# Gate rows broadcast from one SBUF partition each instead of from DRAM

## The chip, the cores and the metric

The kernel runs on one core of a Trainium2 chip. The metric is device microseconds (us) from launch to end, the median of three runs. A profile is of one further execution, whose own time is given beside its span.

## The reference, cut to what matters

One decoder block on 512 tokens of width 1024, float32, 8 heads of 128 in each of two branches:

```python
u = rmsnorm(x, norm_mix_g)
proj = u @ w_in                       # q,k,v,z,a,b | q,k,v,f | gate_a, gate_b
# branch A: gated delta rule in chunks of 64
beta = sigmoid(gb);  g = -exp(a_log) * softplus(ga + dt_bias);  G = cumsum(g) in a chunk
decay[c, s] = exp(G[c] - G[s])                   (s <= c)
a_mat       = beta[c] * (k k^T) * decay          (s < c), inverted with 1 on the diagonal
attn_intra  = (q k^T) * decay;   q_dec = q * exp(G)
# branch B: softmax attention with a forget bias
cum = cumsum(log_sigmoid(ff + f_bias));  s = q k^T / sqrt(d) + cum[t] - cum[s]
merged = sigmoid(gate_a) * (o_a @ P_A) + sigmoid(gate_b) * (o_b @ P_B)
h = x + merged @ w_out;  out = h + relu(rmsnorm(h) @ w_up)^2 @ w_down
```

Four scalars per head and token come out of the gates: exp(G), beta, G (taken from the middle of a block of 128 tokens), and minus the running sum of the forget logs. Each of them is wanted in two forms: as a column (one value a partition, tokens on partitions), and as a row of 512 tokens that stands the same on all 128 partitions. The rows are what this case is about.

## The kernel before, in words

Every float32 product is made of three fast passes: a matrix is split into a rounded part `hi` (on ScalarE) and a remainder `lo` (on VectorE), and TensorE adds hi*hi, hi*lo and lo*hi. All weights come from DRAM in units of 128x1024 (512 KB), are split on arrival, and are used once. Three buffers hold raw units (`wraw`), four hold the split ones (`whl`); a unit is loaded three ahead of its use, and its load waits until the `lo` of the unit three before it has been computed.

The work before the MLP runs in this order on TensorE: the gate and z projections; for heads 0 to 3 of branch A three projections a head (`project`), with the work of the heads (`head`) between them; projections of branch B (`fox_pair`); heads 4 to 7 of branch A; a stream of the remaining projections. Block inverses, the scan over chunks and the softmax attention (`fox_worker`) are spread between these as coroutines. The order of instructions on each engine is fixed at build time by a scheduler.

The rows. `gates` computes the four scalars as columns in the tile `rows`, [128, 4, 4, 8] (kind, block of 128 tokens, head). One TensorE transpose turns kinds 0 to 2 into [96, 128], one turns kind 3 into [32, 128]; VectorE copies them to SBUF (`rowsT`, `rowsF`), and two DMAs, one on POOL's queue and one on SP's, write them to a DRAM tensor `rowd` [4, 4, 8, 128]. `row_page(kind, h)` then fills a [128, 512] page with one row: a DMA on SP's queue reads the four pieces of 128 values (512 bytes each) from DRAM once for each partition. There are 32 such transfers of 256 KB. Four buffers (`rwp`) hold them.

Who uses a row. In `decays`, rows of kind 2 and 1 of a head are fetched one head ahead: POOL masks kind 2 into `em`, ScalarE takes the exponential of it, POOL multiplies it by kind 1 into `eb`. In `head`, VectorE multiplies k k^T by `eb` (line 642) and k q^T by `em` (line 651), and POOL multiplies q by the row of kind 0 (line 653). `fox_worker` masks the row of kind 3 on POOL.

SP's queue carries, in its fixed order, the weight units, these rows, and the stores of the heads' results to DRAM (`hd`) and their reads back.

Of the kernel before, what the change touches and what calls it, by code (L numbers as in the profile page):

```python
# [7 lines left out]
F32 = mybir.dt.float32  # L8
F32R = mybir.dt.float32r
AF = mybir.ActivationFunctionType  # L10
ALU = mybir.AluOpType
# [4 lines left out]
P = 128  # L16
T = 512
D = 1024
KT = D // P
H = 8  # L20
NCH = T // P
# [22 lines left out]
def hybrid_block(tc, a, out):  # L44
    nc = tc.nc
# [6 lines left out]
    drp = ctx.enter_context(tc.tile_pool(name="drp", bufs=1, space=DRAM))  # L52
    mix = ExitStack()
    cm = mix.enter_context(tc.tile_pool(name="cm", bufs=1))
    rwp = mix.enter_context(tc.tile_pool(name="rwp", bufs=4))
# [10 lines left out]
    def nm(s):  # L66
        n_names[0] += 1
        return f"{s}_{n_names[0]}"
# [5 lines left out]
    def page(dt=F32, s="pg"):  # L74
        if s in FOX_TAGS:
            return fxp.tile([P, T], dt, tag=s, name=nm(s))
        tag = TAGS_OF.get(s, s)
        if tag in TAGS:
            return pgp.tile([P, T], dt, tag=tag, name=nm(s), bufs=TAGS[tag])
        return pgp.tile([P, T], dt, tag="pg", name=nm(s))  # L80
# [3 lines left out]
    def const(shape, s, dt=F32):  # L84
        return (cp if s in KEEP else cm).tile(shape, dt, tag=s, name=s)
# [15 lines left out]
    def atps(s="at"):  # L101
        return pat.tile([P, T], F32, tag="at", name=nm(s))

    def v3(ap, n):
        return ap.rearrange("p (a b) -> p a b", a=n)

    def bc(ap, n):
        return ap.unsqueeze(2).to_broadcast(list(ap.shape) + [n])

    def cs(c):  # L110
        return slice(c * P, (c + 1) * P)

    mm = nc.tensor.matmul
    vec, act, pool = nc.vector, nc.scalar, nc.gpsimd
# [23 lines left out]
    def start(gen):  # L138
        tasks.append(gen)
        return gen  # L140
# [160 lines left out]
    ident = const([P, P], "ident")  # L301
# [52 lines left out]
    def inv_rms(pss, rs, rb):  # L354


        for c in range(NCH):
            vec.tensor_scalar(rs[:, c:c + 1], pss[:, c * 64:c * 64 + 1], 1.0 / D, EPS, op0=ALU.mult, op1=ALU.add)
        rsq(rs, rs)
        yield  # L360
        prb = atps("rb")
        for c in range(NCH):
            mm(prb[:, cs(c)], rs[:, c:c + 1].to_broadcast([P, P]), ident, start=True, stop=True)
        act.copy(rb, prb)
# [21 lines left out]
    for pool_, tag, n in early:  # L386
        t = pool_.tile([P, n * T], F32R, tag=tag, name=nm("xs"))
# [22 lines left out]
    def normalise():  # L410
        for k in range(KT):
            pool.tensor_tensor(xt[k], xt[k], rb, op=ALU.mult)
            split(xt[k], mix_g[:, k:k + 1], dst=(uh(k), ul(k)))
            nc.sync.dma_start(ud[k], xt[k])
            if k % 2:
                yield
# [38 lines left out]
    beta = const([P, NCH, H], "beta")  # L455
    gf = const([P, NCH, 16], "gf")
    ngc = const([P, NCH, H], "ngc")
    kds = const([P, NCH, H], "kds")
    dec = const([P, NCH, H], "dec")
    nbe = const([P, NCH, H], "nbe")  # L460
    cc = const([P, NCH, H], "cc")
    rowd = drp.tile([4, NCH, H, P], F32, tag="rowd", name="rowd")

    def rowc(t):
        return t[:, :].unsqueeze(1).to_broadcast([P, NCH, H])

    def gates(ps):
        abT = page(s="abT")
        act.copy(abT[:64, :], ps[:64, :])
        yield from inv_rms(pss, rs, rb)  # L470
        start(normalise())
        yield
        pt = atps("abt")
        for c in range(NCH):
            mm(pt[:, c * 32:(c + 1) * 32], abT[:64, cs(c)], blk_id[0:64, :], start=True, stop=True)
        ab = const([P, NCH, 32], "ab")
        vec.tensor_tensor(ab, v3(pt[:, 0:NCH * 32], NCH), bc(rs[:, :], 32), op=ALU.mult)
        act.activation(beta, ab[:, :, 8:16], AF.Exp, scale=-1.0)
        aexp = const([P, H], "aexp")
        act.activation(aexp, alog, AF.Exp)  # L480
        yy = const([P, NCH, 16], "yy")
        vec.tensor_tensor(yy[:, :, 0:8], ab[:, :, 0:8], rowc(dtb), op=ALU.add)
        vec.tensor_tensor(yy[:, :, 8:16], ab[:, :, 16:24], rowc(fbias), op=ALU.add)
        vec.tensor_scalar(yy[:, :, 8:16], yy[:, :, 8:16], -1.0, None, op0=ALU.mult)

        ee = const([P, NCH, 16], "ee")
        vec.scalar_tensor_tensor(ee, yy, -1.0, yy, op0=ALU.mult, op1=ALU.min)
        act.activation(ee, ee, AF.Exp)
        yield
        vec.tensor_scalar(beta, beta, 1.0, None, op0=ALU.add)  # L490
        vec.reciprocal(beta, beta)
        zz = const([P, NCH, 16], "zz")
        vec.tensor_scalar(zz, ee, 2.0, None, op0=ALU.add)
        vec.reciprocal(zz, zz)
        vec.tensor_tensor(zz, zz, ee, op=ALU.mult)
        vec.tensor_tensor(ee, zz, zz, op=ALU.mult)
        pp = const([P, NCH, 16], "pp")
        vec.tensor_scalar(pp, ee, 1.0 / 19, None, op0=ALU.mult)
        for k in (17, 15, 13, 11, 9, 7, 5, 3):
            vec.scalar_tensor_tensor(pp, pp, 1.0 / k, ee, op0=ALU.add, op1=ALU.mult)  # L500
        vec.scalar_tensor_tensor(pp, pp, 1.0, zz, op0=ALU.add, op1=ALU.mult)
        vec.tensor_scalar(yy, yy, 0.0, None, op0=ALU.max)
        vec.scalar_tensor_tensor(gf, pp, 2.0, yy, op0=ALU.mult, op1=ALU.add)
        vec.scalar_tensor_tensor(gf[:, :, 0:8], gf[:, :, 0:8], -1.0, rowc(aexp), op0=ALU.mult, op1=ALU.mult)
        vec.tensor_scalar(gf[:, :, 8:16], gf[:, :, 8:16], -1.0, None, op0=ALU.mult)
        yield
        pc = atps("cum")
        mm(pc[:, 0:64], upper, gf[:, :, :].rearrange("p a b -> p (a b)"), start=True, stop=True)
        mm(pc[:, 64:128], ones, gf[:, :, :].rearrange("p a b -> p (a b)"), start=True, stop=True)
        cum = const([P, NCH, 16], "cum")  # L510
        vec.tensor_copy(cum, v3(pc[:, 0:64], NCH))
        mm(pc[:, 128:160], mid, gf[:, :, 0:8], start=True, stop=True)
        tot = const([P, NCH, 16], "tot")
        vec.tensor_copy(tot, v3(pc[:, 64:128], NCH))

        rows = const([P, 4, NCH, H], "rows")
        vec.tensor_copy(rows[:, 2], v3(pc[:, 128:160], NCH))
        act.activation(rows[:, 0], cum[:, :, 0:8], AF.Exp)
        vec.tensor_copy(rows[:, 1], beta)
        pt = atps("rowsT")  # L520
        nc.tensor.transpose(pt[:96, 0:P], rows[:, 0:3, :, :].rearrange("p k c h -> p (k c h)"), ident)
        rowsT = const([96, P], "rowsT")
        vec.tensor_copy(rowsT, pt[:96, 0:P])
        nc.gpsimd.dma_start(rowd[0:3, :, :, :].rearrange("k c h t -> (k c h) t"), rowsT)
        vec.tensor_scalar(ngc, rows[:, 2], -1.0, None, op0=ALU.mult)
        yield
        early_rows[0] = True
        vec.tensor_copy(cc[:, 0], cum[:, 0, 8:16])
        pre = const([P, NCH, H], "pre")
        vec.tensor_copy(pre[:, 1], tot[:, 0, 8:16])  # L530
        for c in range(2, NCH):
            vec.tensor_tensor(pre[:, c], pre[:, c - 1], tot[:, c - 1, 8:16], op=ALU.add)
        vec.tensor_tensor(cc[:, 1:], cum[:, 1:, 8:16], pre[:, 1:], op=ALU.add)
        vec.tensor_scalar(rows[:, 3], cc, -1.0, None, op0=ALU.mult)
        vec.tensor_tensor(kds, tot[:, :, 0:8], cum[:, :, 0:8], op=ALU.subtract)
        act.activation(kds, kds, AF.Exp)
        act.activation(dec, tot[:, :, 0:8], AF.Exp)
        vec.scalar_tensor_tensor(nbe, beta, -1.0, rows[:, 0], op0=ALU.mult, op1=ALU.mult)
        yield
        pt = atps("rowsT")  # L540
        nc.tensor.transpose(pt[:32, 0:P], rows[:, 3, :, :].rearrange("p c h -> p (c h)"), ident)
        rowsF = const([32, P], "rowsF")
        vec.tensor_copy(rowsF, pt[:32, 0:P])
        nc.sync.dma_start(rowd[3, :, :, :].rearrange("c h t -> (c h) t"), rowsF)

    def row_tile(src, v=None):
        t = rwp.tile([P, T], F32, tag="row", name=nm("row"))
        nc.sync.dma_start(v3(t[:, :], NCH) if v else t, src)
        return t

    def row_page(kind, h):
        return row_tile(rowd[kind, :, h, :].partition_broadcast(P), True)


    G = 4
# [57 lines left out]
    def head(h, AT, q, k, v, box, res):  # L613
# [27 lines left out]
        for c in range(NCH):  # L641
            vec.scalar_tensor_tensor(AT[:, hi_ * NCH + c, :], pkk[:, cs(c)], r2[:, c:c + 1], eb[:, cs(c)],
                                     op0=ALU.mult, op1=ALU.mult)
        er = row_page(0, h)
        yield
        pkq = atps("kq")
# [214 lines left out]
    def bias_rows(n):  # L861

        if n < len(fq) and n not in rows_of:
            rows_of[n] = row_page(3, fq[n][0])
        return rows_of.get(n)
# [525 lines left out]
    for k, (w, c, p, s_) in enumerate(MLP):  # L1391
# [6 lines left out]
        n = pos[0]  # L1398
# [122 lines left out]
```

## Time and profile before

| | |
|---|---|
| three runs | 977.39, 977.97, 980.99 us; median 977.97 |
| profiled execution | 979.09 us, span 977.3 us, TensorE clock 1.00 |
| TensorE matmuls | 968.0 us busy, 99% of the span |
| VectorE, ScalarE, GpSimd (POOL) | 73%, 63%, 22% |
| DMA | 176.50 MB, mean 181 GB/s |
| row transfers from DRAM | 32, issued from 69.7 to 358.5 us |

A share is over the whole span, so what counts for the rows is the stretch in which they are fetched: 14 of the 32 are issued between 69 and 121 us, while the first four heads are worked on, and eight between 245 and 272 us, when the second four begin. TensorE's busy time includes the pipelining of matmuls and says whether it had something under way, not how far it is from its peak.

### The profile page before, as it was taken

What the parts mean: (1) busy time and instruction counts of PE and PEld (TensorE: products, weight loads), DVE (VectorE), ACT (ScalarE), POOL (GpSimd) and SP (SyncE); (2) the same over time, 40 slices, a digit from 0 to 9 for tenths busy, and PEclk for the clock granted to TensorE, in tenths of its full rate; (3) what the DMA queues carried; (4) which work ended last, traced back from release to release, by engine and by line L of the source; (5) the groups of instructions that cost most, each with busy time, mean ns of one, the idle gap of its engine ahead of it and who ended that gap; (6) DMA issues with size and microseconds to landing.
All of it is one profiled execution on the core that took longest, in us unless ns stands there. A gap on an engine that the chain in (4) does not pass through costs nothing.

```text
span 977.3 us, 17204 instructions
## 1 busy us (share of the span) xinstructions
PE 968.0 (99%) x6532; PEld 871.9 (89%) x6532; DVE 709.4 (73%) x1206; ACT 617.8 (63%) x1079; POOL 219.5 (22%) x220
## 2 busy tenths in 40 slices
PE   8999999999999999999999999999999999999998
PEld 6788899998888999999998888889989989988986
DVE  6877777656577799855656534889896697698596
ACT  7778654766764787868567412668755765666761
POOL 1503220202313423521320014412121121121110
PEclk9999999999999999999999999999999999999999
DMA  7646872475675987757888726678698888889883
GB/s 267 210 146 191 236 179 88 130 256 175 156 210 163 194 155 169 174 120 175 252 172 234 258 88 191 113 180 173 184 197 192 194 168 203 184 170 205 187 175 110
DMA packets 97634, 176.50 MB, mean 181 GB/s; under 512 B 8160, under 2 KB 53376, under 8 KB 97552
## 3 DMA queue, kind: packets, MB, share of 16 engines
q1 hardware_dynamic: 83088, 122.92, 40.6%
q0 software_dynamic: 14464, 52.49, 30.8%
q8 instruction: 51, 0.84, 0.4%
q14 instruction: 31, 0.25, 0.1%
HBM read 154.34 MB, written 21.04 MB: 179 GB/s over the span
## 4 chain that ended last, share of the span: by engine, by line
PE 91%; ACT 3%; DVE 2%; issue 2%; DMA 1%; POOL 0%; SPq 0%; ACTq 0%; POOLq 0%; DVEq 0%
PE mlp L1172 36%; PE st L1012 13%; PE mm L279 7%; PE mm L276 7%; PE mm L275 7%; PE fx L965 2%; PE fx L962 2%; PE fx L963 2%; PE fo L945 2%; PE sc L920 2%; PE pT L936 1%; ACT hi L256 1%; PE kq L648 1%; PE kk L640 1%; DMA row<-oad 1%
## 5 line engine op out<-in xcount | busy, mean ns | idle before, releaser
L1403 ACT CAST hi<-draw 128x1024 fp32r<-128x1024 f32 x124 | 130.1, 1050 | 118.4 <-PE mlp L1172 101.5
L1410 DVE TENSOR_TENSOR lo<-draw,hi 128x1024 fp32r<-128x1024 f32 x124 | 151.2, 1221 | 44.9 <-ACT hi L1403 42.1
L256 ACT CAST hi<-raw 128x1024 fp32r<-128x1024 f32 (+1 forms) x62 | 62.7, 1020 | 77.6 <-PE mm L276 48.6
L1172 PE MATMUL mlp<-hi,shi 128*128 128x512 f32 x280 | 109.5, 391 | 0.1
L1172 PE MATMUL mlp<-hi,slo 128*128 128x512 f32 x280 | 109.1, 390 | 0.0
L1172 PE MATMUL mlp<-lo,shi 128*128 128x512 f32 x280 | 109.0, 389 | 0.0
L257 DVE TENSOR_TENSOR lo<-raw,hi 128x1024 fp32r<-128x1024 f32 (+1 forms) x62 | 75.4, 1222 | 28.3 <-ACT hi L256 13.6
L1172 PE MATMUL mlp<-slo,hi 128*128 128x256 f32 x448 | 90.3, 283 | 0.0
L1172 PE MATMUL mlp<-shi,lo 128*128 128x256 f32 x448 | 90.3, 283 | 0.0
L1172 PE MATMUL mlp<-shi,hi 128*128 128x256 f32 x448 | 90.3, 283 | 0.0
L276 PE MATMUL mm<-ulo,hi 128*128 128x512 f32 x216 | 84.9, 394 | 1.2 <-DVE ulo L290 1.2
L275 PE MATMUL mm<-uhi,hi 128*128 128x512 f32 x216 | 85.2, 396 | 0.0
L257 DVE TENSOR_TENSOR lo<-sraw,hi 128x1024 fp32r<-128x1024 f32 x49 | 61.6, 1257 | 23.5 <-ACT hi L256 20.1
L1172 PEld LDWEIGHTS mlp<-shi,hi 128*128 128x128 f32 x448 | 70.6, 192 | 0.9
L256 ACT CAST hi<-sraw 128x1024 fp32r<-128x1024 f32 x49 | 51.3, 1047 | 30.7 <-PE st L1012 14.8
L1172 PEld LDWEIGHTS mlp<-shi,lo 128*128 128x128 f32 x448 | 69.9, 192 | 0.0
L1172 PEld LDWEIGHTS mlp<-slo,hi 128*128 128x128 f32 x448 | 69.8, 192 | 0.0
L1172 PEld LDWEIGHTS mlp<-hi,shi 128*128 128x128 f32 x280 | 52.6, 188 | 11.1 <-issue 0.7
L1172 PEld LDWEIGHTS mlp<-lo,shi 128*128 128x128 f32 x280 | 52.6, 188 | 11.1
L1172 PEld LDWEIGHTS mlp<-hi,slo 128*128 128x128 f32 x280 | 52.6, 188 | 10.3
L600 DVE SCALAR_TENSOR_TENSOR conv<-mm,c_conv,conv 128x511 f32<-128x511 f32 (+2 forms) x72 | 53.5, 744 | 5.6 <-ACT conv L597 4.4
L279 PE MATMUL mm<-uhi,lo 128*128 128x512 f32 x216 | 57.1, 402 | 0.0
(337 smaller groups left out, 2389.7 us busy)
## 6 DMA issues: line engine op xcount, KB each, us to landing
draw<-w_u POOLq DMA_DIRECT2D x32, 512.0 KB, 6.0
draw<-w_d POOLq DMA_DIRECT2D x32, 512.0 KB, 6.0
sraw<-w_st POOLq DMA_DIRECT2D x28, 512.0 KB, 6.0
draw<-w_d SPq DMA_DIRECT2D x26, 512.0 KB, 4.3
raw<-w_gdn SPq DMA_DIRECT2D x24, 512.0 KB, 4.3
draw<-w_u SPq DMA_DIRECT2D x24, 512.0 KB, 4.5
sraw<-w_st SPq DMA_DIRECT2D x21, 512.0 KB, 5.2
hd<-hd SPq DMA_DIRECT2D x34, 256.0 KB, 5.5
```

What stands on the lines that cost most here:

```text
L256: act.copy(hi[:, c], raw[:, c])
L257: vec.tensor_tensor(lo[:, c], raw[:, c], hi[:, c].bitcast(F32), op=ALU.subtract)
L275: mm(o, w, rhi(k), start=(k == 0), stop=False)
L276: mm(o, w, rlo(k), start=False, stop=False)
L279: mm(o, lo[:, k * cols:(k + 1) * cols], rhi(k), start=False, stop=(k == KT - 1))
L600: vec.scalar_tensor_tensor(y[:, s:], ps[:, :T - s], cw[:, i:i + 1], y[:, s:], op0=ALU.mult, op1=ALU.add)
L920: mm(psc[:, :n], qT[:, s], kT[:, :n], start=True, stop=True)
L945: mm(po[:, cs(i)], vt[c], st[i][:, cs(c)], start=(c == 0), stop=(c == i))
L1012: mm(o, u, w, start=first and t == 0 and k == 0 and j == 0 and x is hi, stop=x is lo and k == 3, skip_group_check=True)
L1172: return (lambda *args, **kw: tc.keep_in_program_order(f(*args, **kw))) if self.pinned[0] else f
L1403: pact.copy(hi, raws[m][0])
L1410: pvec.tensor_tensor(lo, raws[m][0], hi[:, :].bitcast(F32), op=ALU.subtract)
```

## The change

Each row becomes one partition of one SBUF tile. `rows` is laid out [128, 4, 32] (block, kind and head); `rows_out` makes four transposes for a set of kinds, one a block, into the four column blocks of one PSUM page, and one VectorE copy brings them to the tile `rowf` [40, 512]: partitions 0 to 23 hold kinds 0 to 2, partitions 32 to 39 kind 3. `row_page` reads a row from its partition of `rowf` with a step of 0 over 128 copies. The DRAM tensor and its two writing DMAs go. The small tiles of `gates` move into one page of the shared page pool, which makes room for `rowf`.

```diff
-    rowd = drp.tile([4, NCH, H, P], F32, tag="rowd", name="rowd")
+    rows = const([P, NCH, 4 * H], "rows")
+    rowf = const([40, T], "rowf")
+
+    def rows_out(kinds, p0):
+        n, k0 = len(kinds) * H, kinds[0] * H
+        pt = atps("rowsT")
+        for c in range(NCH):
+            nc.tensor.transpose(pt[:n, cs(c)], rows[:, c, k0:k0 + n], ident)
+        vec.tensor_copy(rowf[p0:p0 + n, :], pt[:n, :])
...
-        ab = const([P, NCH, 32], "ab")
+        tmp = page(s="gates")
+        ab = v3(tmp[:, 0:P], NCH)
+        yy, ee, zz, pp, cum, tot = [v3(tmp[:, P + 64 * i:P + 64 * i + 64], NCH) for i in range(6)]
...
-        pt = atps("rowsT")
-        nc.tensor.transpose(pt[:96, 0:P], rows[:, 0:3, :, :].rearrange("p k c h -> p (k c h)"), ident)
-        rowsT = const([96, P], "rowsT")
-        vec.tensor_copy(rowsT, pt[:96, 0:P])
-        nc.gpsimd.dma_start(rowd[0:3, :, :, :].rearrange("k c h t -> (k c h) t"), rowsT)
+        rows_out((0, 1, 2), 0)
...
-        pt = atps("rowsT")
-        nc.tensor.transpose(pt[:32, 0:P], rows[:, 3, :, :].rearrange("p c h -> p (c h)"), ident)
-        rowsF = const([32, P], "rowsF")
-        vec.tensor_copy(rowsF, pt[:32, 0:P])
-        nc.sync.dma_start(rowd[3, :, :, :].rearrange("c h t -> (c h) t"), rowsF)
+        rows_out((3,), 32)
...
     def row_page(kind, h):
-        return row_tile(rowd[kind, :, h, :].partition_broadcast(P), True)
+        n = (kind if kind < 3 else 4) * H + h
+        t = rwp.tile([P, T], F32, tag="row", name=nm("row"))
+        nc.sync.dma_start(t, rowf[n:n + 1, :].unsqueeze(1).to_broadcast([1, P, T]))
+        return t
```

On SP's queue, where the first rows are fetched, there stood before (`rowd` is the DRAM tensor, `raw` a weight unit, `hd` a store of a head's results):

```order
L227 DMA raw_903<-w_gdn 128x1024
L544 DMA rowd<-rowsF 32x128
L548 DMA row_616<-rowd 128x4x128
L548 DMA row_618<-rowd 128x4x128
L548 DMA row_818<-rowd 128x4x128
L548 DMA row_820<-rowd 128x4x128
L227 DMA raw_983<-w_gdn 128x1024
L148 DMA hd_592<-kn_748 128x4x128
```

and stands now (`rowf` is the SBUF tile):

```order
L227 DMA raw_899<-w_gdn 128x1024
L549 DMA row_612<-rowf 128x1x512
L549 DMA row_614<-rowf 128x1x512
L549 DMA row_814<-rowf 128x1x512
L549 DMA row_816<-rowf 128x1x512
L227 DMA raw_979<-w_gdn 128x1024
L148 DMA hd_588<-kn_744 128x4x128
L148 DMA hd_588<-vb_798 128x4x128
```

The write to DRAM is gone from the queue; the rows keep their places between the weights and the stores, here and in the rest of the queue. On POOL's queue the other write (`rowd<-rowsT`) is gone and nothing else has moved.

On TensorE, in the projection before the first rows (`mm` is that product, `ktm` the first head's transposes), there stood before:

```order
L276 MATMUL mm_714<-ulo_190,hi_634 128x512
L521 MATMUL rowsT_471<-ident,rows 96x128
L275 MATMUL mm_714<-uhi_183,hi_634 128x512
L276 MATMUL mm_714<-ulo_191,hi_634 128x512
L275 MATMUL mm_714<-uhi_184,hi_634 128x512
L276 MATMUL mm_714<-ulo_192,hi_634 128x512
L541 MATMUL rowsT_539<-ident,rows 32x128
L119 MATMUL ktm_731<-ident,conv_665 128x128 x4
```

and stands now:

```order
L276 MATMUL mm_710<-ulo_190,hi_630 128x512
L469 MATMUL rowsT_465<-ident,rows 24x128 x4
L275 MATMUL mm_710<-uhi_183,hi_630 128x512
L469 MATMUL rowsT_534<-ident,rows 8x128 x4
L276 MATMUL mm_710<-ulo_191,hi_630 128x512
L275 MATMUL mm_710<-uhi_184,hi_630 128x512
L276 MATMUL mm_710<-ulo_192,hi_630 128x512
L119 MATMUL ktm_727<-ident,conv_661 128x128 x4
```

Eight transposes stand where two stood, all before the same head's transposes.

More of the change, by code (lines that the diff above doesn't have):

```diff
@@ L480, in gates @@
         act.activation(aexp, alog, AF.Exp)
-        yy = const([P, NCH, 16], "yy")
         vec.tensor_tensor(yy[:, :, 0:8], ab[:, :, 0:8], rowc(dtb), op=ALU.add)
@@ L484, in gates @@
         vec.tensor_scalar(yy[:, :, 8:16], yy[:, :, 8:16], -1.0, None, op0=ALU.mult)
-        ee = const([P, NCH, 16], "ee")
         vec.scalar_tensor_tensor(ee, yy, -1.0, yy, op0=ALU.mult, op1=ALU.min)
@@ L491, in gates @@
         vec.reciprocal(beta, beta)
-        zz = const([P, NCH, 16], "zz")
         vec.tensor_scalar(zz, ee, 2.0, None, op0=ALU.add)
@@ L496, in gates @@
         vec.tensor_tensor(ee, zz, zz, op=ALU.mult)
-        pp = const([P, NCH, 16], "pp")
         vec.tensor_scalar(pp, ee, 1.0 / 19, None, op0=ALU.mult)
@@ L509, in gates @@
         mm(pc[:, 64:128], ones, gf[:, :, :].rearrange("p a b -> p (a b)"), start=True, stop=True)
-        cum = const([P, NCH, 16], "cum")
         vec.tensor_copy(cum, v3(pc[:, 0:64], NCH))
         mm(pc[:, 128:160], mid, gf[:, :, 0:8], start=True, stop=True)
-        tot = const([P, NCH, 16], "tot")
         vec.tensor_copy(tot, v3(pc[:, 64:128], NCH))
[L516 to L519, printed above, removed]
-        pt = atps("rowsT")
-        nc.tensor.transpose(pt[:96, 0:P], rows[:, 0:3, :, :].rearrange("p k c h -> p (k c h)"), ident)
-        rowsT = const([96, P], "rowsT")
-        vec.tensor_copy(rowsT, pt[:96, 0:P])
-        nc.gpsimd.dma_start(rowd[0:3, :, :, :].rearrange("k c h t -> (k c h) t"), rowsT)
-        vec.tensor_scalar(ngc, rows[:, 2], -1.0, None, op0=ALU.mult)
+        vec.tensor_copy(rows[:, :, 2 * H:3 * H], v3(pc[:, 128:160], NCH))
+        act.activation(rows[:, :, 0:H], cum[:, :, 0:8], AF.Exp)
+        vec.tensor_copy(rows[:, :, H:2 * H], beta)
+        rows_out((0, 1, 2), 0)
+        vec.tensor_scalar(ngc, rows[:, :, 2 * H:3 * H], -1.0, None, op0=ALU.mult)
         yield
@@ L533, in gates @@
         vec.tensor_tensor(cc[:, 1:], cum[:, 1:, 8:16], pre[:, 1:], op=ALU.add)
-        vec.tensor_scalar(rows[:, 3], cc, -1.0, None, op0=ALU.mult)
+        vec.tensor_scalar(rows[:, :, 3 * H:], cc, -1.0, None, op0=ALU.mult)
         vec.tensor_tensor(kds, tot[:, :, 0:8], cum[:, :, 0:8], op=ALU.subtract)
@@ L537, in gates @@
         act.activation(dec, tot[:, :, 0:8], AF.Exp)
-        vec.scalar_tensor_tensor(nbe, beta, -1.0, rows[:, 0], op0=ALU.mult, op1=ALU.mult)
+        vec.scalar_tensor_tensor(nbe, beta, -1.0, rows[:, :, 0:H], op0=ALU.mult, op1=ALU.mult)
         yield
-        pt = atps("rowsT")
-        nc.tensor.transpose(pt[:32, 0:P], rows[:, 3, :, :].rearrange("p c h -> p (c h)"), ident)
-        rowsF = const([32, P], "rowsF")
-        vec.tensor_copy(rowsF, pt[:32, 0:P])
-        nc.sync.dma_start(rowd[3, :, :, :].rearrange("c h t -> (c h) t"), rowsF)
+        rows_out((3,), 32)
     def row_tile(src, v=None):
```

## The prediction

> **What bounds the kernel now.** I read the page's list of busy times first, then the waits, then the stretches in which rows are fetched.
>
> ```profile
> PE 968.0 (99%) x6532; PEld 871.9 (89%) x6532; DVE 709.4 (73%) x1206; ACT 617.8 (63%) x1079; POOL 219.5 (22%) x220
> PE 91%; ACT 3%; DVE 2%; issue 2%; DMA 1%; POOL 0%; SPq 0%; ACTq 0%; POOLq 0%; DVEq 0%
> ```
>
> TensorE has something under way for 968.0 of 977.3 us, and the chain of waits stands on it for 91%. A cheaper row can shorten the kernel only where TensorE waits for a row, or for something behind one. TensorE's list of waits, longest first, begins so:
>
> ```profile
> PE mm L276 <- DVE ulo L290: 1.2, 2, 0.7
> PE mm L402 <- ACT xs L289: 1.1, 2, 0.6
> PE warm L305 <- DVE expo L300: 1.1, 1, 1.1
> ```
>
> Nothing in it is longer, and nothing of it hangs on a row. So there is next to nothing to win, and the question is what cover the row transfers have. The stretches of 10 us in which the first heads are worked on (engine columns, then the clock, the share of the DMA engines' time, GB/s):
>
> ```profile
> core 0: us, PE busy (x) PEld busy (x) DVE busy (x) ACT busy (x) POOL busy (x), PEclk, DMA share, GB/s
> 70.00:80.00 10.00, 10.00 (x51) 8.39 (x51) 7.20 (x14) 7.98 (x27) 1.91 (x3) 1.00 0.33 99
> 90.00:100.00 10.00, 10.00 (x56) 8.55 (x55) 7.73 (x15) 8.54 (x19) 5.70 (x6) 1.00 0.91 202
> 110.00:120.00 10.00, 10.00 (x56) 8.53 (x55) 8.52 (x20) 3.04 (x6) 0.97 (x2) 1.00 0.89 238
> ```
>
> TensorE is full throughout, but the DMA engines reach 0.9. What stands on SP's queue there, from the DMA issues of 69 to 121 us (count, size, median us to landing), with the rates in 40 slices of that stretch:
>
> ```profile
> GB/s 57 58 87 65 71 86 158 149 130 143 161 295 310 347 183 238 93 138 231 207 348 225 201 138 182 330 313 243 118 147 215 334 344 308 147 63 113 220 374 393
> row<-rowd SPq DMA_DIRECT2D x14, 256.0 KB, 8.8
> raw<-w_fox SPq DMA_DIRECT2D x6, 512.0 KB, 8.5
> ```
>
> The weights that TensorE needs stand in one queue with 14 rows. How near they already are to being late, ScalarE's waits from 60 to 130 us say, and then the wait in its timeline; behind it VectorE's remainder of that unit and TensorE's first use of the pair of units that it belongs to:
>
> ```profile
> ACT hi L256 <- DMA raw<-w_fox: 6.9, 2, 5.5
> 120.67 1.05 ACT L256 CAST hi<-raw 128x1024 fp32r<-128x1024 f32 x1 [5.46 <-DMA raw<-w_fox]
> 121.75 1.23 DVE L257 TENSOR_TENSOR lo<-raw,hi 128x1024 fp32r<-128x1024 f32 x1 [1.16 <-ACT hi L256]
> 134.70 0.36 PE L962 MATMUL fx<-hi,uhi 128*128 128x256 f32 x1
> ```
>
> ScalarE stood 5.46 us for that weight. Its split ended at 121.75 + 1.23 = 122.98, TensorE takes it up at 134.70: 11.7 us of cover are left, and no more. That figure is the hinge of the whole case.
>
> **The change part by part.** *The row transfer* is the part that counts, 32 times. What it takes now: in 70:80 the four first rows are all but alone on the queue, 99 GB/s x 10 us = 0.99 MB, 3.8 rows of 0.262 MB, or 2.6 us a row, with the engines only a third busy. The changed one moves the same 256 KB to the same 128 partitions in 128 pieces of 2 KB instead of 512 of 512 bytes, which by itself could only be quicker. But all 128 pieces are read from one partition, and no row of this trace reads so. Bounds, from the nearest rows:
>
> ```profile
> out<-acc SPq DMA_DIRECT2D x8, 256.0 KB, 2.0
> rowd<-rowsF SPq DMA_DIRECT2D x1, 16.0 KB, 1.5
> ```
>
> Below: `out<-acc` reads 256 KB of SBUF out of all 128 partitions, and takes 2.0 us where 16 KB take 1.5, so 0.5 us for the bytes. That is the price if a partition can be read as fast as all of them together. Above: the best rate of the slices, 393 GB/s, is what 16 engines get together; if one partition gives no more than one engine's share, 393 / 16 = 24.6 GB/s, a row takes 262 KB / 24.6 = 10.7 us.
>
> [...]
>
> Between 0.5 and 10.7 I take the upper mechanism, since 128 reads of the same bytes differ from `out<-acc` in just that, but with two rows under way at a time: rows next to each other on the queue come from different partitions (kind 2 of head 0 from 16, kind 1 from 8, then 17 and 9), and the queue has several transfers in flight, as 8.8 us to landing at 2.6 us a row shows. That is 10.7 / 2 = 5.3 us a row, 2.7 more than now.
>
> *First heads.* The late weight above was issued at 112.36; these are the first and the last rows issued ahead of it, 14 in all:
>
> ```profile
> 69.71 2.04 SPq L548 DMA_DIRECT2D row<-rowd  x4
> 110.26 2.01 SPq L548 DMA_DIRECT2D row<-rowd  x1
> 112.36 0.64 SPq L227 DMA_DIRECT2D raw<-w_fox  x1
> ```
>
> 14 x 2.7 = 37.8 us later, less 11.7 of cover: TensorE stands 26.1 us. The rows themselves are as late, and POOL already waits for them (its waits on rows, all the run: 7.7 for `conv`, 6.4 for `em`, 3.7 for `eb`):
>
> ```profile
> POOL conv L653: 7.7, 2
> POOL em L583: 6.4, 4
> POOL eb L589: 3.7, 1
> ```
>
> Behind a late `eb` VectorE stands at line 642, with the next `lo` and the convolutions queued behind it. This runs beside the late weights, in the same queue and by the same amount, so I count the larger alone.
>
> *Second heads.* From 245.8 to 271 us eight rows are issued. The first and the last of them, and the stretches:
>
> ```profile
> 245.84 0.46 SPq L548 DMA_DIRECT2D row<-rowd  x1
> 271.06 0.36 SPq L548 DMA_DIRECT2D row<-rowd  x1
> ...
> 240.00:260.00 20.00, 20.00 (x106) 17.08 (x105) 8.22 (x10) 11.81 (x20) 8.56 (x8) 1.00 0.55 159
> 260.00:280.00 20.00, 19.87 (x101) 16.35 (x100) 13.57 (x21) 17.53 (x40) 4.88 (x5) 1.00 0.84 208
> ```
>
> 8 x 2.7 = 21.6 us more, against 20 x (0.45 + 0.16) = 12.2 us in which the DMA engines have nothing to do, and the same 11.7 of cover, since the weights run equally far ahead: 0. The other 10 rows stand about 18 us apart or more, but for a last pair: 0.
>
> *The detour through DRAM* goes. Its two writes took 1.9 us (`rowsT`) and 1.5 us (`rowsF`, above) to land, and the first row was issued 1.3 us after the second:
>
> ```profile
> rowd<-rowsT POOLq DMA_DIRECT2D x1, 48.0 KB, 1.9
> L524 POOL DMA_DIRECT2D rowd<-rowsT x1: 629/629/629, 67.8 to 67.8; - x1
> L544 SPq DMA_DIRECT2D rowd<-rowsF x1: 339/339/339, 68.4 to 68.4; - x1
> L521 PE MATMUL rowsT<-ident,rows x1: 272/272/272, 64.8 to 64.8; 128*96 128x128 f32 x1
> L523 DVE COPY rowsT<-rowsT x1: 277/277/277, 67.2 to 67.2; 96x128 f32<-96x128 f32 x1
> ```
>
> About 1 us earlier for the first row, which the longer copies take back: 512 columns instead of 128 at 277 ns, at most 4 x 0.28 = 1.1 us for each of two, on VectorE, which is 72% busy there. Were that cover gone, it would be 1.7 us. *Transposes:* six more on TensorE, in a stretch where it is full. One is 0.27 us alone; in a row of its kind it takes less, as eight matmuls of 128x128 on the chain show:
>
> ```profile
> 78.43 0.89 PE kk L640 x8
> ```
>
> 0.89 / 8 = 0.11, so 6 x 0.11 = 0.7 us on the path. *The gates' small tiles in one page:* the same instructions on other addresses, 0; one page of 53 is held until the gates are done, and the order on the engines shows nothing that moved for it.
>
> The sum, on the profiled execution's 979.09 us: 979.1 + 26.1 + 0.7 = 1005.9. That execution lies 1.1 us above the median of the runs, so 1005 us.
>
> **The rivals.** *One row after the other.* If the engines take a queue's pieces strictly in order, the second partition is not read before the first is done, and a row costs 10.7 us, 8.1 more. First heads 14 x 8.1 - 11.7 = 101.7; second 8 x 8.1 - 12.2 - 11.7 = 40.9; in all 979.1 + 101.7 + 40.9 + 0.7 - 1.1 = 1121 us. For it: 16 engines with eight pieces each, all at one door. Against it: a queue that already has three or four transfers in flight. [...]
>
> *No limit at one partition.* If 2.6 us come from the number of pieces (the engines are a third busy at 512 pieces a row), and a partition is read as fast as needed, 128 pieces take a quarter, about 0.7 us, and the queue empties. TensorE was not waiting, so nothing is won by it: 979.1 + 0.7 - 1.1 = 979 us. This side decides up to a price of 2.6 + 11.7 / 14 = 3.4 us a row, the point at which the cover is used up. For it: the low share in 70:80. Against it: the reads all go to one place.
>
> *Faster* than that would need time that TensorE now loses where the rows are fetched:
>
> ```profile
> 60.00:380.00 320.00, 319.87 (x2306) 289.90 (x2306) 233.14 (x516) 211.09 (x453) 80.06 (x73) 1.00 0.66 175
> ```
>
> It is idle for 320.00 - 319.87 = 0.13 us there; 5 us would have to come from elsewhere, and I see no place.
>
> **How the numbers follow.** Half a per cent, 5 us, is about what a measurement of this kernel tells from no change. The bounded price with rows overlapping, 1005, anywhere from 988 to 1040: 0.42. One after the other, 1040 to 1121: 0.30. No limit, 973 to 983: 0.24, of which 0.20 within half a per cent and 0.04 faster. The last 0.04 is for a small loss between 983 and 988. So faster 0.04, same 0.20, slower 0.42 + 0.30 + 0.04 = 0.76. The range runs from 976, the no-limit case, to 1090, most of the serial one, and leaves out less than 2 in 10. The forecast's own range is 988 to 1040.
>
> **What would show it.** Right: rows that land over 15 us after issue in the first heads, with the engines' share near 1 at a rate of under 100 GB/s; ScalarE's casts (line 256) waiting for `raw` for tens of us; TensorE waiting between 80 and 140 us and hardly from 240 to 280; the rest of the span as long as before. Rival one: DMA-bound in both stretches, some 40 us lost in the second. Wrong altogether: landings under 5 us, and TensorE full from 70 to 130 us.

## The result, and the profile after

The changed kernel takes 1118.49 us (median of 4 runs, 1112.95 to 1119.34), the kernel before 978.17 us beside it: a ratio of 1.1417, 95% interval 1.1373 to 1.1461. The prediction had the direction, but 140 us are lost where it had 27, and the time lies outside its range. The profiled execution took 1117.67 us, with a span of 1115.9.

Busy times, the granted clock in 40 slices, and the chain of waits by engine and by line, of the changed kernel:

```profile
PE 995.6 (89%) x6538; PEld 892.1 (80%) x6538; DVE 705.9 (63%) x1206; ACT 616.3 (55%) x1079; POOL 218.3 (20%) x219
PEclk9998685899998789898999999999999999999999
PE 67%; DMA 19%; DVE 6%; ACT 4%; SPq 2%; issue 1%; POOL 0%; ACTq 0%; POOLq 0%; DVEq 0%
PE mlp L1170 31%; PE st L1010 9%; DMA row<-rowf 9%; DMA sraw<-w_st 4%; PE mm L279 4%; PE mm L276 4%; PE mm L275 4%; DMA raw<-w_fox 3%; PE fx L960 2%; PE fx L961 2%; PE fx L963 2%; DVE conv L598 1%; DMA hd<-kn 1%; DVE lo L257 1%; PE fo L943 1%
```

TensorE was 99% busy and is 89% busy. Transfers were 1% of the chain and are 19%, first among them the rows, then two kinds of weights. Two things happened to TensorE: it stands idle 1115.9 - 995.6 = 120.3 us where it stood 9.3, and the same work keeps it busy 27.6 us longer (968.0 to 995.6), at a granted clock that falls below full speed from 84 to 223 us and again from 335 to 530.

Where in the program it is lost shows in the last start of three groups of TensorE's matmuls (the two times are the first and the last start): `fx` ends the stretch of the first heads, `kk` that of the second heads, `mlp` is the last stage. Before:

```profile
L962 PE MATMUL fx<-hi,uhi x192: 277/283/368, 121.1 to 210.3; 128*128 128x256 f32 x192
L640 PE MATMUL kk<-conv x64: 270/275/275, 78.3 to 338.6; 128*128 128x128 f32 x64
L1172 PE MATMUL mlp<-hi,shi x280: 387/389/487, 616.9 to 972.7; 128*128 128x512 f32 x140
```

After:

```profile
L960 PE MATMUL fx<-hi,uhi x192: 278/283/562, 159.6 to 288.2; 128*128 128x256 f32 x192
L638 PE MATMUL kk<-conv x64: 270/275/421, 78.1 to 452.4; 128*128 128x128 f32 x64
L1170 PE MATMUL mlp<-hi,shi x280: 387/389/487, 755.4 to 1111.2; 128*128 128x512 f32 x140
```

At the end of the first heads the kernel is 288.2 - 210.3 = 77.9 us late, at the end of the second 113.8 (35.9 more), when the last stage begins 138.5 (24.7 more), and at its end still 138.5. The same three stretches by engine, before and then after (TensorE's busy time is the first number behind the length; the clock and the DMA engines' share stand last but two and last but one):

```profile
60.00:210.30 150.30, 150.30 (x1226) 138.55 (x1226) 106.30 (x241) 96.73 (x207) 31.13 (x28) 1.00 0.61 174
210.30:338.60 128.30, 128.17 (x752) 111.64 (x751) 89.60 (x178) 81.87 (x182) 37.88 (x34) 1.00 0.68 179
338.60:616.90 278.30, 277.83 (x2096) 255.93 (x2095) 178.52 (x358) 167.80 (x308) 71.92 (x65) 1.00 0.69 178
```

```profile
60.00:288.20 228.20, 159.04 (x1229) 144.53 (x1229) 104.78 (x240) 96.23 (x207) 30.91 (x27) 0.84 0.80 113
288.20:452.40 164.20, 138.07 (x753) 118.19 (x751) 85.81 (x175) 78.43 (x177) 37.01 (x34) 0.91 0.86 128
452.40:755.40 303.00, 285.43 (x2095) 262.66 (x2094) 179.66 (x361) 170.18 (x311) 71.93 (x65) 0.97 0.70 169
```

In the first stretch TensorE is idle for 228.20 - 159.04 = 69.2 us, and its own work is 159.04 - 150.30 = 8.7 us longer; in the second 26.1 and 9.9, in the third 17.6 and 7.6. The DMA engines are busier while they move less: 0.80 at 113 GB/s where it was 0.61 at 174.

Two of the stretches of 10 us that the prediction showed of before, now:

```profile
70.00:80.00 10.00, 10.00 (x52) 8.40 (x51) 7.69 (x14) 6.28 (x22) 2.33 (x2) 1.00 0.91 37
90.00:100.00 10.00, 1.91 (x9) 1.25 (x7) 5.15 (x10) 3.26 (x6) 1.63 (x1) 0.73 0.88 127
```

In the first, the four first rows are fetched: 99 GB/s at a share of 0.33 has become 37 GB/s at 0.91. TensorE still has work then; from 90 to 100 us it has 1.91 us of it.

The transfers of 69 to 210 us (share of the 16 engines in tenths, GB/s in 40 slices of 3.5 us, then the rows and one kind of weights with the median us to landing):

```profile
DMA  9897797899898987998989879899999889889999
GB/s 31 26 55 35 73 50 72 209 86 27 184 30 82 51 25 170 34 37 158 31 26 192 31 137 52 25 28 27 27 150 53 25 217 43 27 136 241 366 120 28
row<-rowf SPq DMA_DIRECT2D x14, 256.0 KB, 18.1
raw<-w_fox SPq DMA_DIRECT2D x7, 512.0 KB, 13.0
```

Eighteen of the 40 slices lie under 40 GB/s (25 to 37, mean 28.9) with the engines' share at 0.7 to 0.9: that is the rate of a row by itself (26 to 28 in runs below). In the slices of 150 and more between them weights and stores move. At 27 GB/s a row of 262 KB takes 9.7 us.

How a late row reaches TensorE, by the waits behind which most is lost. ScalarE's waits for two weights, one after the other, and behind the second TensorE's for ScalarE:

```profile
177.15 1.04 ACT L256 CAST hi<-raw 128x1024 fp32r<-128x1024 f32 x1 [26.43 <-DMA raw<-w_fox]
198.44 1.04 ACT L256 CAST hi<-raw 128x1024 fp32r<-128x1024 f32 x1 [19.13 <-DMA raw<-w_fox]
199.39 0.63 ACT L600 ACTIVATE conv<-conv 128x512 f32<-128x512 f32 x1
200.07 1.12 PE L119 MATMUL ktm<-ident,conv 128*128 128x128 f32 x4 [37.34 <-ACT conv L600]
```

and the chain of waits between 60 and 240 us, three of its longest pieces (start, us, what):

```profile
68.47 18.93 DMA row<-rowf
...
153.75 23.33 DMA raw<-w_fox
...
184.61 13.75 DMA raw<-w_fox
```

The rows hold POOL, which masks them (`em`, `eb`, with waits of up to 9.10 and 9.81 us for a row in the first heads); ScalarE's exponentials follow POOL; the weights stand on SP's queue among the rows, and ScalarE, whose order is fixed, stands at a cast (line 256) with the activation of the next head's `conv` (line 600) behind it: VectorE's part of that `conv` (line 598) had ended at 181.06 + 1.52 = 182.58 us, and the activation began at 199.39. TensorE stops at that head's transposes (`ktm`), not at the projection that the weight is for. In the third stretch the chain runs through the weights `w_st`. Late rows are on their way at the same time on SP's queue, but only the second of these three weights was issued there; the first and the third were issued on POOL's queue, which carries no rows:

```profile
442.63 16.23 DMA sraw<-w_st
...
472.47 12.47 DMA sraw<-w_st
...
488.95 21.14 DMA sraw<-w_st
```

### The profile page after: what moved, and what is told of

Its sections match the earlier page's. It is cut to its first block, busy times and chain, and to the rows that moved or that the text cites. A ratio compares the mean times of both kernels' runs of the same rounds, so it can differ in the third digit from the quotient of the medians.

```text
span 1115.9 us, 17208 instructions
## 1 busy us (share of the span) xinstructions
PE 995.6 (89%) x6538; PEld 892.1 (80%) x6538; DVE 705.9 (63%) x1206; ACT 616.3 (55%) x1079; POOL 218.3 (20%) x219
## 4 chain that ended last, share of the span: by engine, by line
PE 67%; DMA 19%; DVE 6%; ACT 4%; SPq 2%; issue 1%; POOL 0%; ACTq 0%; POOLq 0%; DVEq 0%
PE mlp L1170 31%; PE st L1010 9%; DMA row<-rowf 9%; DMA sraw<-w_st 4%; PE mm L279 4%; PE mm L276 4%; PE mm L275 4%; DMA raw<-w_fox 3%; PE fx L960 2%; PE fx L961 2%; PE fx L963 2%; DVE conv L598 1%; DMA hd<-kn 1%; DVE lo L257 1%; PE fo L943 1%
## 5 line engine op out<-in xcount | busy, mean ns | idle before, releaser
L256 ACT CAST hi<-raw 128x1024 fp32r<-128x1024 f32 (+1 forms) x62 | 62.7, 1020 | 135.1 <-DMA raw<-w_fox 51.8
L119 PE MATMUL ktm<-ident,conv 128*128 128x128 f32 x32 | 6.9, 355 | 69.9 <-ACT conv L600 69.9
L279 PE MATMUL mm<-uhi,lo 128*128 128x512 f32 x216 | 66.1, 451 | 0.0
L119 PEld LDWEIGHTS ktm<-ident,conv 128*128 128x128 f32 x32 | 4.8, 179 | 72.0 <-ACT conv L600 71.6
```

The source lines that it names most:

```text
L256: act.copy(hi[:, c], raw[:, c])
L279: mm(o, lo[:, k * cols:(k + 1) * cols], rhi(k), start=False, stop=(k == KT - 1))
```

## The experiments

Each kernel is the changed one with the edit shown; lines that only declare tiles or lay out the transposes are left out. Ratios are to the kernel before on the same chip.

**Is it the source partition?** Everything of the change stays, the piece size of 2 KB too, but the tile is written to DRAM and the rows are read from there.

```diff
-        vec.tensor_copy(rowf[p0:p0 + n, :], pt[:n, :])
+        vec.tensor_copy(rowf[p0:p0 + n, :], pt[:n, :])
+        (nc.sync if p0 else nc.gpsimd).dma_start(rowd[p0:p0 + n, :], rowf[p0:p0 + n, :])
...
-        nc.sync.dma_start(t, rowf[n:n + 1, :].unsqueeze(1).to_broadcast([1, P, T]))
+        nc.sync.dma_start(t, rowd[n, :].partition_broadcast(P))
```

> The change with one thing undone: rowf (40 rows of 2 KB) is written to DRAM, and each row is read from there, in 128 pieces of 2 KB. Transposes, the page of the gates and the size of the pieces stay as in the change; only the source is DRAM again. If the one source partition is the cause: within 5 us of the kernel before (978), the first four rows at 2.6 us each or less. If the size or number of the pieces, or one of the other edits, costs the time: 1100 us or more.

Measured: 978.99 us, ratio 1.0006 (0.9997 to 1.0016). The first rows while nothing else moves, in the kernel before and then in this one:

```profile
71.00:77.00 6.00, 6.00 (x30) 4.97 (x29) 4.58 (x11) 4.00 (x14) 1.69 (x2) 1.00 0.29 79
```

```profile
72.00:76.00 4.00, 4.00 (x21) 3.30 (x20) 2.84 (x8) 2.75 (x12) 2.59 (x2) 1.00 0.58 137
```

So the six transposes, the layout of the gates and the new page cost nothing that can be measured, and the whole loss is in reading one partition. The run says a second thing: at 137 GB/s a row takes 262 KB / 137 = 1.9 us where the kernel before, with 512-byte pieces at 79 GB/s, pays 3.3, and nothing is won by it, as TensorE was not waiting. (The prediction's 2.6 us come from 70 to 80 us, in which the first pieces of a weight move too. The 0.8 us that two expectations below give a row of this kernel is the rate of 76 to 78 us, 325 GB/s, of which a part is a weight as well.)

**Has each partition a limit of its own?** Each row is laid on 16 partitions, and its 128 reads are spread over them: on neighbours (16 h to 16 h + 15), or 8 apart (h, h + 8, ...). POOL makes the copies ahead of the transposes; three pages fewer make room.

```diff
+            x = page(s="rowx")
+            pool.tensor_copy(x[:, :].rearrange("p (c h j) -> p c h j", c=NCH, h=H),
+                             rows[:, :, kind * H:(kind + 1) * H].unsqueeze(3).to_broadcast([P, NCH, H, 16]))
+            vec.tensor_copy(rowp[kind], transposes(x, "rowsT"))
...
+        nc.sync.dma_start(t, rowp[kind][h * 16:(h + 1) * 16, :].unsqueeze(1).to_broadcast([16, H, T]))
```

The second has `c j h` for `c h j`, with the copies in the other dimension, and reads `rowp[kind][h:P:H, :]`.

> Each row stands on 16 neighbouring partitions of a tile of its kind, and is read as 16 partitions x 8 copies, so each DMA engine reads a partition of its own. (POOL spreads the columns first, 50 shared pages instead of 53.) If each partition has a limit of its own, the 16 together give 393 GB/s as at best before: a row takes 0.7 us, TensorE is full, 980 us. [...] If any broadcast out of SBUF is slow, however many partitions hold the row: 1100 us or more.

> As the run with neighbouring copies, but the 16 copies of a row stand 8 partitions apart. If partitions have limits of their own: the same as with neighbours. [...] If any broadcast out of SBUF is slow: 1100 us or more.

Measured: 995.60 us (ratio 1.0172, 1.0147 to 1.0197) and 987.73 us (1.0103, 1.0086 to 1.012). Two us in which rows alone are fetched, of the first and then of the second:

```profile
72.00:74.00 2.00, 2.00 (x10) 1.65 (x9) 2.00 (x4) 0.63 (x2) 0.00 (x0) 1.00 0.91 103
```

```profile
72.00:74.00 2.00, 2.00 (x10) 1.65 (x10) 2.00 (x5) 0.28 (x1) 0.00 (x0) 1.00 1.01 205
```

Both times lie between what was expected of partitions with limits of their own (980 us) and of a broadcast that is slow from any number of them (1100 or more). Sixteen partitions each time, and yet 103 GB/s for neighbours and 205 for spread ones. A limit of each partition by itself would give both the same; it falls. Against the 27 GB/s of one partition the two are 3.8 and 7.6 times as much, and both lie below the 393 that moved at best before: some of the sixteen hold each other back, neighbours more than those 8 apart. That each DMA engine reads a partition of its own was the author's estimate; no trace shows which engine reads which piece.

**What the spreading itself costs.** The kernel with the copies 8 apart still lost 9.5 us, so its control keeps the copies, the pages and the transposes, and reads the rows from DRAM:

```diff
+            nc.sync.dma_start(rowd[kind], rowp[kind][0:H, :])
...
+        nc.sync.dma_start(t, rowd[kind, h, :].partition_broadcast(P))
```

> Control for e3_copies_far: the same spreading on POOL, the same 16 transposes and 50 pages, but the rows are read from DRAM in pieces of 2 KB (written there from the first copy). If the 9.5 us that e3_copies_far loses come from the spreading and the order of work around it: 984 to 990 us, as e3. If they come from reading 16 partitions: 978 to 981 us.

Measured: 988.69 us, ratio 1.0113 (1.0088 to 1.0139), the same loss. The 20 us ahead of the first rows, of the kernel before and then of the control:

```profile
40.00:60.00 20.00, 18.80 (x85) 14.91 (x84) 18.35 (x39) 14.73 (x19) 1.80 (x2) 1.00 0.57 176
```

```profile
40.00:60.00 20.00, 16.13 (x74) 12.36 (x73) 17.10 (x44) 9.84 (x15) 4.60 (x6) 1.00 0.44 144
```

TensorE has done 2.7 us less work there before any row is fetched, and in the profiles the first `kk` starts 5.8 us later than before (84.1 against 78.3), the last stage 6.8 (623.7 against 616.9). So the spreading and the order of work around it cost most of the time ahead of the first use of a row, and rows out of sixteen copies 8 apart cost nothing that shows beside rows from DRAM (987.73 and 988.69 us). Which part of the spreading does it (pages, POOL's copies, the transposes) was not taken apart.

**Which rows run side by side?** The three kinds of rows that the first heads need get places of their own. In the first kernel, kinds 2 and 1 of a head lie on partitions h and 32 + h, in the second on h and 64 + h. Kind 0 takes the place that is left, 64 + h and then 32 + h; else they are the same. So rows next to each other in the first pairs come from partitions 32 apart in the one and 64 apart in the other.

```diff
+    SLOT = (64, 32, 0, 96)
...
-        n = (kind if kind < 3 else 4) * H + h
+        n = SLOT[kind] + h
```

The second has `SLOT = (32, 64, 0, 96)`.

> The change with other partitions: kind 2 of head h on partition h, kind 1 on 32 + h, kind 0 on 64 + h, kind 3 on 96 + h (12 small copies and 14 more transposes, some 2 us). [...]

> [...]

Measured: 1142.08 us (ratio 1.1663, 1.1636 to 1.1689) and 1117.29 us (1.1416, 1.1399 to 1.1433). Both have eight transposes and two copies more than the change, fewer than the expectation says. POOL's second and third wait for a row in its timeline, and 12 us of rows alone, of the first kernel and then of the second:

```profile
89.89 1.29 POOL L588 TENSOR_TENSOR eb<-em,row 128x512 f32<-128x512 f32 x1 [9.24 <-DMA row<-rowf]
99.60 0.63 POOL L582 TENSOR_SCALAR_AFFINE_SELECT em<-row 128x512 f32<-128x512 f32 x1 [8.42 <-DMA row<-rowf]
77.00:89.00 12.00, 12.00 (x66) 10.16 (x65) 4.14 (x6) 7.91 (x11) 0.64 (x1) 1.00 0.91 28
```

```profile
85.98 1.29 POOL L588 TENSOR_TENSOR eb<-em,row 128x512 f32<-128x512 f32 x1 [5.48 <-DMA row<-rowf]
89.14 0.92 POOL L582 TENSOR_SCALAR_AFFINE_SELECT em<-row 128x512 f32<-128x512 f32 x1 [1.86 <-DMA row<-rowf]
77.00:89.00 12.00, 12.00 (x65) 10.21 (x64) 6.10 (x11) 7.91 (x11) 1.93 (x2) 1.00 0.79 56
```

On h and 32 + h a row follows the other by 99.60 - 89.89 = 9.7 us; on h and 64 + h the third is there 3.2 us after the second, which overlapped it, and the rate is 56 GB/s instead of 28. So the overlap that the prediction assumed exists between neighbours in the queue, but not for every pair of partitions; and over the whole kernel it is worth 24.8 us of 164. The changed kernel, whose neighbours in the queue come from partitions 16, 8, 17 and 9, stands where the second one does.

**Is it the queue?** Kind 1 on POOL's queue, and in another kernel all rows there, so that SP's holds only weights and stores:

```diff
-        nc.sync.dma_start(t, rowf[n:n + 1, :].unsqueeze(1).to_broadcast([1, P, T]))
+        (nc.gpsimd if kind == 1 else nc.sync).dma_start(t, rowf[n:n + 1, :].unsqueeze(1).to_broadcast([1, P, T]))
```

The second has `nc.gpsimd.dma_start` for all kinds.

> The change, with the rows of kind 1 issued on POOL's queue instead of SP's; the others stay. If rows of different partitions are not read at the same time because one queue's pieces are taken in order, then two queues read two partitions at once: the first 10 us of rows run at 55 GB/s instead of 30, the first stretch loses half as much, 1040 to 1075 us. If an engine serves one piece at a time whatever queue it is from: 30 GB/s again and 1100 to 1125 us.

> The change with all 32 rows issued on POOL's queue, so SP's queue has the weights and stores alone and no weight stands behind a row. If TensorE loses its time to weights that queue behind rows: the first and second heads are nearly whole again, 985 to 1020 us. If the rows' own lateness is enough (14 rows at 8.7 us against 52 us of work), or if the engines hold back other queues' pieces too: 1090 us or more.

Measured: 1111.28 us (ratio 1.1353, 1.1335 to 1.1372) and 1099.82 us (1.1236, 1.1206 to 1.1266). What moved in the first, by queue (q1 is SP's, q0 POOL's; packets, MB, share of the 16 engines), from 69 to 78 us and then from 79 to 89:

```profile
q1 hardware_dynamic: 115, 0.24, 84.6%
```

```profile
q0 software_dynamic: 91, 0.32, 89.8%
q1 hardware_dynamic: 115, 0.19, 9.1%
```

and in the second 10 us of rows beside a weight on the other queue, the landing of that kind of weights over 69 to 210 us, and ScalarE's longest wait from 60 to 300 us:

```profile
69.00:79.00 10.00, 10.00 (x50) 8.25 (x49) 6.35 (x13) 7.79 (x23) 4.20 (x5) 1.00 0.87 26
```

```profile
raw<-w_gdn SPq DMA_DIRECT2D x2, 512.0 KB, 30.3
```

```profile
ACT hi L256 <- DMA raw<-w_fox: 39.8, 3, 34.8
```

In the first kernel POOL issued its rows at 68.86 us, but until 78 us nothing of them moved: SP's queue alone had the engines, 0.24 MB in 9 us, 27 GB/s. From 79 to 89 us rows of both queues move, 0.51 MB in 10 us, 51 GB/s. So rows of two queues do run side by side once both are taken up; why the second queue had to wait for 10 us is left open. Within a queue the rows next to each other now come from neighbouring partitions (16 and 17 on SP's, 8 and 9 on POOL's), and these do not: SP's first two, issued from 68.57 us on, moved at the 27 GB/s of one. In the second kernel the 26 GB/s are rows alone, and weights that share no queue with a row take 30.3 us to land (the two of `w_gdn`; the eleven of `w_fox`, most of them issued later, 6.6 in the median). The rows hold the 16 engines (a share of 0.87 at 26 GB/s), not the queue, and moving them wins back 7 to 19 of 140 us. How much of the 121.5 us that are still lost in the second comes from such weights, and how much from the rows' own lateness, this run does not tell.

**How many such rows can be borne?** Kinds 1 and 2 from the tile and the others from DRAM; then kind 1 alone.

```diff
+        if kind in (1, 2):
+            nc.sync.dma_start(t, rowf[n:n + 1, :].unsqueeze(1).to_broadcast([1, P, T]))
+        else:
+            nc.sync.dma_start(t, rowd[n, :].partition_broadcast(P))
```

The second has `kind == 1`.

> A dose: of the 32 rows only kinds 1 and 2 (16 rows) come from their one partition at 8.7 us a row; kinds 0 and 3 come from DRAM in pieces of 2 KB at 0.8 us, as in e1. By the queue's sum, first heads 8 x (8.7 - 2.6) - 6 x 1.8 - 11.7 of cover = 26 us; second heads 8 x 6.1 - 12.2 - 11.7 = 25 us: 1030 us, from 1015 to 1045. If the loss went with the number of rows alone, half of 140: 1048 us.

> A smaller dose: only kind 1 (8 rows, one a head) from its partition, the rest from DRAM in pieces of 2 KB. By the queue's sum, first heads 4 x 6.1 - 10 x 1.8 - 11.7 is below 0, second heads 4 x 6.1 - 4 x 1.8 - 12.2 - 11.7 is below 0: all covered, 978 to 985 us. If each such row costs TensorE its share of the 140 us (4.4 each): 1013 us.

Measured: 1024.24 us (ratio 1.0461, 1.0444 to 1.0479), within its range, and 994.61 us (1.0163, 1.0148 to 1.0179), which neither theory had. Sixteen rows of 32 cost 46 us and all of them 140: the loss grows faster than the number. With 8 rows, though, a loss is there already. In that kernel, POOL's wait for a row out of DRAM, and TensorE's longest wait from 60 to 600 us:

```profile
98.18 1.27 POOL L656 TENSOR_TENSOR conv<-conv,row 128x512 f32<-128x512 f32 x1 [11.56 <-DMA row<-rowd]
```

```profile
PE vtm L119 <- ACT conv L605: 9.8, 3, 5.0
```

The cheap row stood behind a slow one: SP took 6.89 us to issue the row from the tile ahead of it and 9.11 for the store behind that, issued this one at 90.16, and it was there 7.88 us later. POOL's order is fixed, and `conv` of the next head, ScalarE's activation of it and TensorE's transposes follow. That way has less cover than the weights.

## Why the prediction was wrong

**Nothing to win: right.** The run with cheaper rows, 1.9 us each, took 978.99.

**The price of a row: the first step that failed.** The prediction took the upper mechanism, a partition that gives no more than one engine's share, at 10.7 us, and halved it "with two rows under way at a time" to 5.3. The price of a row alone was near: 27 GB/s, 9.7 us. The mechanism was an estimate that no run shows: the 16 engines together stood at a share of 0.91 with 28 GB/s of rows, and at 1.01 with 205 from sixteen copies 8 apart, so that one engine's share, 24.6 GB/s, lies so near may be luck. The halving did not hold for all rows. It held where rows stand next to each other on the queue and come from partitions 64 apart (56 GB/s; 28 from partitions 32 apart); further on a row stands alone between weights and stores, as the 18 slices under 40 GB/s show. What the 14 rows cost on average shows in the weight that the prediction's sum is about: ScalarE's cast of it began at 120.67 us and begins at 198.44 now, 77.8 us or 14 x 5.6 later, where the sum had 14 x 2.7 = 37.8. On the prediction's 2.6 us that is 8.2 us a row. "8.8 us to landing at 2.6 us a row" had been taken as several rows in flight, but a queue with several transfers in flight does not mean that their reads proceed together: with partitions 32 apart four rows were issued from 67.30 us on, and they moved at 28 GB/s.

**The cover of 11.7: the second step that failed.** The split of that weight ends at 200.74 us now (its `lo` starts at 199.51 and takes 1.23), and TensorE takes up that pair of units here:

```profile
212.52 0.36 PE L960 MATMUL fx<-hi,uhi 128*128 128x256 f32 x1
```

That is 11.8 us later: the cover is still there, and the delay went past it. TensorE stood at `ktm` instead, whose `conv` ScalarE activates right behind the late cast (198.44, 199.39 and 200.07 above). So nothing comes off the 77.8.

**First heads: 26.1 forecast, 77.9 measured.** Of the 51.8 missed, 40 are the price (77.8 - 37.8) and 11.7 the cover. "I count the larger alone" was weak too: rows and weights were both late in every run, and no run held back one without the other, so what either would do by itself stays open. In the kernels with fewer such rows this account holds only roughly. With 5.6 more for a row from its partition and 1.4 less (3.3 - 1.9) for one from DRAM, kinds 1 and 2 give 8 x 5.6 - 6 x 1.4 = 36.4, and `fx` ended 29.7 us late; kind 1 gives 4 x 5.6 - 10 x 1.4 = 8.4, and it was 10.3. The expectation for kinds 1 and 2 came near with 0.8 us for a row from DRAM, where the trace shows 1.9, and with 11.7 off for a cover that the changed kernel left untouched.

**Second heads: 0 forecast, 35.9 measured.** With 5.6 more a row and no cover the prediction's form gives 8 x 5.6 - 12.2 = 32.6. **"The other 10 rows: 0": 24.7 measured**, through `w_st` beside late rows, two of which SP took 9.46 us to issue. Both zeros rested on the halved price, the first on the cover too.

**Not in the sum at all: TensorE's own work grew by 27.6 us.** Two groups of the same 216 matmuls, before and after (busy us, mean ns):

```profile
L279 PE MATMUL mm<-uhi,lo 128*128 128x512 f32 x216 | 57.1, 402 | 0.0
```

```profile
L279 PE MATMUL mm<-uhi,lo 128*128 128x512 f32 x216 | 66.1, 451 | 0.0
```

The granted clock of the changed kernel in a stretch that was all wait:

```profile
180.00:200.00 20.00, 0.00 (x0) 0.00 (x0) 4.07 (x12) 1.56 (x3) 0.00 (x0) 0.50 0.92 130
```

In the three stretches the clock went with the idle time: 0.84 with 69.2 us idle of 228.2, 0.91 with 26.1 of 164.2, 0.97 with 17.6 of 303.0, and before, with 0.5 us or less in each, 1.00. Here a stall cost its own length and then slower matmuls: 27.6 us beside 111 us of added idle time, about a quarter on top.

**Transposes, the longer copies, the gates' page: right.** The DRAM run holds them all, at +0.8 us.

**The rivals.** "One row after the other", 1121 us and a chance of 0.30, was nearest, but its agreement within 3 us is luck. Its mechanism is only half that of the runs: rows that stand apart go one after the other, neighbours from partitions 64 apart do not (56 GB/s), and the kernel in which the neighbours of the first pairs, 32 apart, go one after the other too (28 GB/s) takes 1142.08. Nor are its terms those measured: it had 101.7 us in the first heads where 77.9 were lost, 40.9 in the second where 35.9 were, nothing in the third where 24.7 were, and no clock. "No limit at one partition" falls with the first run. The chances were wrong between the first two: what spoke against the serial case was a depth of queue, which says nothing of where the reads meet.

**What would show it.** Rows landing over 15 us after issue (18.1), the engines' share near 1 under 100 GB/s (the slices above), casts waiting tens of us (26.43) and TensorE waiting between 80 and 140 us all came; so did the 40 us in the second stretch that were named as the sign of the rival. What did not come is the rest of the span as long as before: TensorE waited on until 200 us, and the third stretch lost 24.7.

## What to carry to other kernels

In these runs the rate of a broadcast out of SBUF went with how many source partitions it has and with which they are: one partition gave 27 GB/s, sixteen neighbours 103, sixteen that lie 8 apart 205. Whoever keeps such a source lays copies 8 partitions apart (though the spreading itself cost some 10 us here), or leaves the row in DRAM (137 GB/s with 2 KB pieces). Read the DMA engines' share together with the GB/s: 0.9 at 27 GB/s was engines held at a slow source, and what else was to move then waited, on either queue (two weights on the other queue 30.3 us). Follow a late transfer through the fixed order of the engine that takes it: what stands behind it there can have less cover than its own result. Do not divide a price by the transfers in flight before a row of the profile shows two of them moving at once, and where TensorE will stall for tens of us, add the slower matmuls that follow (27.6 us beside 111 us of idle time here).

## What the runs showed of the hardware

- While rows alone moved: a row from one partition 26 to 28 GB/s, also with the next row 1 or 32 partitions away; two rows from partitions 64 apart 56, two rows on two queues 51; 16 neighbouring copies 103, 16 copies 8 apart 205; DRAM with 2 KB pieces 137, with 512-byte pieces 79.
- Rows from one partition kept the 16 engines at a share of about 0.9 (0.87 at 26 GB/s, 0.91 at 28), and two weights on another queue took 30.3 us to land.
- SP itself is held: issuing the first four rows took 16.71 us after the change and 2.04 before, and what SP issued next, a weight, came at 84.70 us, right behind them. What holds the issue was not looked into.

```profile
67.88 16.71 SPq L549 DMA_DIRECT2D row<-rowf  x4
```
